# Channel sums of bonus and variance in the recurrent groups: two products with rounded parts in place of one full 32-bit product

## The chip, the cores and the metric

The kernel runs on one core of a Trainium2 chip. The metric is the device time of one execution in microseconds (us). Five engines work side by side, each through a queue of its own in a fixed order: TensorE (PE, matrix products; its weight loads are listed as PEld), VectorE (DVE), ScalarE (ACT), GpSimd (POOL), and SyncE (SP), which here only issues DMAs. Semaphores tie them together.

## The reference, cut to what matters

One decoder layer over 1024 tokens of 1024 channels, all in 32-bit floats: three token mixers on one projection, gates, and a gated feed-forward part with a convolution. The change lies in the recurrent mixer, with 16 heads of 64 channels:

```python
y = rwkv7_scan(rh, wh, kh, vh, -kk, kk * ah)
mu = jnp.mean(y, axis=-1, keepdims=True)
var = jnp.mean(jnp.square(y - mu), axis=-1, keepdims=True)
y = ((y - mu) * lax.rsqrt(var + LNX_EPS)).reshape(B, S, RWKV_WIDTH)
y = y * ln_x_w.astype(f32) + ln_x_b.astype(f32)
bonus = jnp.sum(rh * kh * r_k.astype(f32), axis=-1, keepdims=True) * vh
y = y + bonus.reshape(B, S, RWKV_WIDTH)
return y.astype(dt) * g
```

Two sums over the 64 channels of a head occur for every token: that of `rh * kh * r_k` (the bonus) and that of the squares of the centred `y` (the variance).

## The kernel before, in words

Channels lie on the 128 partitions, tokens along the free axis, so a tile holds two heads, and a sum over a head's channels that is spread back to all of them is a matrix product with `bonesr`, a 128x128 matrix of ones in two 64x64 blocks. It is written once as rounded floats (type fp32r, `FR`). `bones` is the same memory read as full 32-bit floats.

Projections use a split. A 32-bit operand is written as a rounded high part (a copy into an fp32r tile) and a low part (the operand less the high part, again fp32r), and `mm3` (L167 to L169) makes three rounded products of the four parts. Weights are split as they arrive: `whi` on ACT (L128), `wlo` on POOL (L131). A projection block is 2 halves of 512 tokens times 8 channel chunks times 3, that is 48 products of 128x512.

The recurrent mixer runs as four groups (0 to 3) of two tiles `i`, four heads, each. In a group `rwkv_group` does the following. (a) It computes gates (`psu`), sums of the squared keys (`square_sums`, tile `sp` in the buffer with tag `NT`, product `phd` with `bonesr`, already in high and low parts), decays, and the scaled keys and queries. (b) Products `ps` between them for all 16 chunks of 64 tokens, copied and masked out of PSUM by ACT and DVE. Between the two tiles' products the function `bonus` is called for both tiles: product `pbo` of `t0_` (the first half of the tile `kv`, in which the products r, k and r_k stand) with the ones, multiplied with the values on DVE (L514), shifted on ACT (L515), written to memory as `d_bv`. Then the scaled keys are transposed (`pt`, L572) into the tile `BKN`, which takes the buffer of `kv` and so must wait until `d_bv` is written. (c) A triangular solve on DVE (L586 to L600), finished on PE (`pz`, `pw`). (d) The scan over 16 chunks, short products (L639) in a chain through DVE and ACT. (e) The next group's keys and values are projected (`group_kv`), and then for each tile the variance: squares on ACT (L706), product `pvar` with the ones (L708), logarithm and exponential on ACT (`rstd`), three DVE operations (L710 to L713), and the result goes to memory as `d_y`.

32 further projection blocks (`fill`) have nothing to do with the groups: their results are spilled, through a staging tile `st` out of a ring of three buffers with tag `st`, to memory, for the stages after the groups. `fill_to` calls them in while a group is being written. Three quarters belong to the groups, eight blocks to the attention stage.

The order in which each engine runs its instructions is set by the scheduler of the Tile framework when the program is built: it takes the instructions as the kernel writes them, the pools' buffers, and waits, and it moves ready projection products in between the others. It is fixed from then on; at run time no engine looks ahead of its queue.

Of the kernel before, what the change touches and what calls it, by code (L numbers as in the profile page):

```python
# [9 lines left out]
F32 = mybir.dt.float32  # L10
FR = mybir.dt.float32r
AF = mybir.ActivationFunctionType
ALU = mybir.AluOpType
# [4 lines left out]
P = 128  # L18
# [5 lines left out]
HALVES = ((0, 512), (512, 512))  # L24
# [20 lines left out]
def trunk_kernel(ctx: ExitStack, tc: tile.TileContext, xT, memT, pvec, w_in, w_kv, w_upd, w_upg,  # L45
                 w_pool, w_ppool, w_pmem, w_prwkv, w_o, w_fup, w_fdn, out):
    nc = tc.nc
    V, A, G, PE, SP = nc.vector, nc.scalar, nc.gpsimd, nc.tensor, nc.sync

    const = ctx.enter_context(tc.tile_pool(name="const", bufs=1))  # L50
    wp = ctx.enter_context(tc.tile_pool(name="wp", bufs=1))
# [22 lines left out]
    def col(name, i):  # L74
        o, w = PV[name]
        return pv[:, o + i:o + i + 1]
# [7 lines left out]
    bonesr = const.tile([P, P], FR, name="bonesr")  # L84
# [2 lines left out]
    G.memset(braw[0:64, 0:64], 1.0)  # L87
    G.memset(braw[64:128, 64:128], 1.0)
    G.tensor_copy(bonesr, braw)
    bones = bonesr.bitcast(F32)  # L90
    cent = const.tile([P, 64], F32, name="cent")
    mstrict = const.tile([P, 64], F32, name="mstrict")
    mincl = const.tile([P, 64], F32, name="mincl")
# [1 line left out]
    for lo in (0, 64):  # L95
        s = slice(lo, lo + 64)
# [3 lines left out]
    for lo in (0, 64):  # L100
        s = slice(lo, lo + 64)
# [18 lines left out]
    def split(src, hi, lo, lo_eng=None):  # L120
        A.copy(hi, src)
        return (lo_eng or V).tensor_tensor(lo, src, hi.bitcast(F32), op=ALU.subtract)
# [80 lines left out]
    def rstd(dst, ps, eps_col, scale=1.0):  # L203
        act(dst, ps, AF.Ln, bias=eps[:, eps_col:eps_col + 1], scale=scale)
        act(dst, dst, AF.Exp, scale=-0.5)
# [9 lines left out]
    rw = rw_ctx.enter_context(tc.tile_pool(name="rw", bufs=1))  # L215
# [7 lines left out]
    for k in range(KC):  # L223
        tag = ("X01", "X11", "HV", "HV")[k // 2]
# [207 lines left out]
    def rwkv_group(g, kv):  # L432
# [13 lines left out]
        for i in range(2):  # L446
            p = 2 * g + i
            uh, ul = load_up2(w_upd[p])
            for t0, _ in HALVES:
                s = slice(t0, t0 + 512)  # L450
                for e, l, dst, b in ((0, ld, tBN[i][:, 0, s], "w0"), (1, la, tHV[:, i, 0, s], "a0")):
                    ps = psg.tile([P, 512], F32, name="psu", tag="g0")
# [7 lines left out]
        def product_bank(name):  # L460

            turn[0] = (turn[0] + 1) % 3
            shape = [P, 4, 2, C]
            return pss.tile(shape, F32, name=name, tag="s") if turn[0] else \
                psk.tile(shape, F32, name=name, tag="k")

        for i in range(2):
            p = 2 * g + i
            t0_, t1_ = kv[i][:, 0], kv[i][:, 1]
# [9 lines left out]
            for t0, _ in HALVES:  # L479
                s = slice(t0, t0 + 512)  # L480
# [26 lines left out]
        def bonus(i):  # L507

            t0_ = kv[i][:, 0]
            for t0, _ in HALVES:  # L510
                s = slice(t0, t0 + 512)
                ps = pss.tile([P, 512], F32, name="pbo", tag="s")
                PE.matmul(ps, bones, t0_[:, s], start=True, stop=True)
                V.tensor_tensor(t0_[:, s], vs[i][:, s], ps, op=ALU.mult)  # L514
            A.activation(t0_, t0_, AF.Identity, bias=col("ln_b", 2 * g + i))  # L515
            SP.dma_start(d_bv[2 * g + i], t0_)
# [4 lines left out]
        NT = rw.tile([P, 2, NCH, C], F32, name="NT", tag="NT")  # L521
        HV = rw.tile([P, 2, NCH, 2, C], F32, name="HV", tag="HV")
        for i in range(2):
            for c0 in (0, 8):
                ps = pss.tile([P, 8, C], F32, name="pv", tag="s")
# [13 lines left out]
        for i in range(2):  # L539
            us = slice(NCH * i, NCH * i + NCH)  # L540
            for c0 in range(0, NCH, 4):
# [4 lines left out]
                ps = product_bank("ps1")  # L546
# [6 lines left out]
                ps = product_bank("ps2")  # L553
# [6 lines left out]
            for b in range(2 if i == 0 else 0):  # L560
                bonus(b)

            n = NCH if i == 0 else 8
# [5 lines left out]
            for c0 in range(0, NCH, 4):  # L569
                ps = pss.tile([P, 4, P], F32, name="pt", tag="s")  # L570
# [18 lines left out]
        for s in range(31):  # L589
            n, m = 31 - s, s + 1  # L590
# [12 lines left out]
        for u0 in (0, 16):  # L603
            us = slice(u0, u0 + 16)
            ps = pss.tile([P, 16, 32], F32, name="pz", tag="s")
# [7 lines left out]
            ps = pss.tile([P, 16, 32], F32, name="pw", tag="s")  # L613
# [7 lines left out]
        for i in range(2):  # L621
            for e in range(2):
                V.tensor_tensor(RB[i][:, e], RB[i][:, e], mincl.unsqueeze(1).broadcast_to([P, NCH, C]),
                                op=ALU.mult)
# [71 lines left out]
        for i in range(2):  # L696
            p = 2 * g + i
            y = AR[:, i, 1]
            gt = rw.tile([P, 2, T], F32, name="gt", tag=tagA[i])
            SP.dma_start(gt[:, 0], d_bv[p])  # L700
            SP.dma_start(gt[:, 1], d_g[p])
            yq = rw.tile([P, T], F32, name="yq", tag=tagC[i])
            for t0, _ in HALVES:
                s = slice(t0, t0 + 512)
                sq = yq[:, s]
                A.activation(sq, y[:, s], AF.Square)  # L706
                ps = pss.tile([P, 512], F32, name="pvar", tag="s")
                PE.matmul(ps, bones, sq, start=True, stop=True)  # L708
                rstd(sq, ps, 2, 1.0 / 64)
                V.tensor_tensor(y[:, s], y[:, s], sq, op=ALU.mult)  # L710
                V.scalar_tensor_tensor(y[:, s], y[:, s], col("ln_w", p), gt[:, 0, s], op0=ALU.mult,
                                       op1=ALU.add)
                V.tensor_tensor(y[:, s], y[:, s], gt[:, 1, s], op=ALU.mult)  # L713
            SP.dma_start(d_y[p], y)
# [17 lines left out]
    for g in range(4):  # L732
        kv = rwkv_group(g, kv)
# [17 lines left out]
    with tc.tile_pool(name="km", bufs=1) as km:  # L751
# [5 lines left out]
        for k in range(KC):  # L757
            sq = km.tile([P, 256], F32, name="msq", tag="msq", bufs=2)
# [24 lines left out]
        for j in range(8):  # L783
            ws = kv_weights(j) if j > 1 else load_w(w_kv[j], KC, c=0)
            ps = gemm(ws, lambda k: (mh[:, k], ml[:, k]), 256)
# [61 lines left out]
    for hd in range(4):  # L847
        for t0, _ in HALVES:
            s = slice(t0, t0 + 512)
# [6 lines left out]
            for u in range(2):  # L856
                ps = psg.tile([P, 2, 256], F32, name="psco", tag="g0")
# [41 lines left out]
    for j in range(8):  # L899
        ws = load_w(w_pmem[j], 4)  # L900
        for n, (t0, _) in enumerate(HALVES):
            s = slice(t0, t0 + 512)
            SP.dma_start(pm[j][n], d_zg[16 + j][:, s])
            act(pm[j][n], pm[j][n], AF.Sigmoid)
            ps = gemm(ws, lambda k: (oh[k][:, s], ol[k][:, s]))
            V.tensor_tensor(pm[j][n], pm[j][n], ps, op=ALU.mult)
    for j in range(8):
# [4 lines left out]
        for n, (t0, _) in enumerate(HALVES):  # L912
            s = slice(t0, t0 + 512)
            ps = gemm(ws, lambda k: (ph_[k][:, s], pl_[k][:, s]))
# [672 lines left out]
```

## Time and profile before

| what | us |
|---|---|
| median of 3 runs (lowest to highest) | 2102.87 (2102.04 to 2109.29) |
| profiled execution, its own time | 2099.71 |
| span of the profiled execution | 2097.7 |
| granted clock of TensorE, mean | 0.992 |
| end of group 3's scan, in the span | 984 |

How to read the rows. A group row is: line, engine, operation, out<-in by the names in the program, shapes, count, then duration in ns as least/median/most, and first and last start in us. A timeline row is: start in us, duration in us, engine, line, operation, tiles, count; in brackets the idle time of the engine before it and what ended that. A row of waits is: who, for whom, us in total, times, longest. PE's products overlap each other in a pipeline: a product's duration is longer than the distance at which the next may start.

### The profile page before, as it was taken

The page shows a single profiled execution, that of the slowest core. Times are in us where ns is not written, and L with a number is a line of the kernel's source. Part 1 is how long each engine was busy: PE and PEld are TensorE (multiplying, and loading weights), DVE is VectorE, ACT ScalarE, POOL GpSimd, SP SyncE. Part 2 cuts the span into 40 slices and gives each one's busy share as a digit, 9 for nine tenths or more (in the row PEclk, how much of TensorE's full clock was granted, in tenths as well). Part 3 has the DMA queues.
Part 4 walks back from the last instruction along what each step waited for, and adds up shares of the span by engine and source line. Part 5 has one row for each costly group of instructions (what it writes and reads, how often), then busy time and mean ns, then how long its engine had stood idle before and what let it go on. Part 6 is the DMA issues. An engine that isn't in the chain of part 4 may idle for free.

```text
span 2097.7 us, 34129 instructions
## 1 busy us (share of the span) xinstructions
PE 2038.1 (97%) x12246; PEld 1564.7 (75%) x12246; DVE 1347.6 (64%) x2159; ACT 1071.2 (51%) x2252; POOL 818.0 (39%) x925
## 2 busy tenths in 40 slices
PE   8999999999999999999999999999999999999997
PEld 5777766776767667776878887777788777777886
DVE  6567437664558346734695542668777777777798
ACT  7585347623763358434566344545444444444644
POOL 5521212121122121111122355555778888842341
PEclk9999999999999999999999999999999999999999
DMA  4312212120212021212526443634322222159776
GB/s 154 128 41 74 66 58 65 61 82 21 86 61 85 30 83 51 80 62 80 199 88 198 143 146 104 217 108 144 97 87 80 75 85 79 61 171 277 167 181 153
DMA packets 176713, 221.83 MB, mean 106 GB/s; under 512 B 16544, under 2 KB 128288, under 8 KB 176544
## 3 DMA queue, kind: packets, MB, share of 16 engines
q1 hardware_dynamic: 163616, 204.44, 30.1%
q0 software_dynamic: 11856, 14.16, 4.2%
q8 instruction: 97, 1.59, 0.3%
q10 hardware_dynamic: 1072, 1.05, 0.1%
q14 instruction: 72, 0.59, 0.1%
HBM read 170.30 MB, written 49.28 MB: 105 GB/s over the span
## 4 chain that ended last, share of the span: by engine, by line
PE 26%; DVE 7%; POOL 6%; DMA 6%; issue 4%; ACT 3%; SPq 1%; POOLq 0%; ACTq 0%; DVEq 0%
PE psg L169 5%; PE psg L167 5%; PE psg L168 5%; POOL wt L1025 3%; PE psd L168 2%; PE psd L169 2%; PE psd L167 2%; POOL wlo L131 2%; PE psf L169 1%; POOL sm L1010 1%; PE psf L168 1%; PE psf L167 1%; DMA a<-in_w_fup 1%; ACT d L1041 1%; DMA R<-d_f 1%
## 5 line engine op out<-in xcount | busy, mean ns | idle before, releaser
L131 POOL TENSOR_TENSOR wlo<-wraw,whi 128x256 fp32r<-128x256 f32 x480 | 420.1, 885 | 953.0 <-ACT whi L128 822.0
L169 PE MATMUL psg<-hh,wlo 128*128 128x512 f32 x928 | 380.7, 410 | 7.4 <-POOL wlo L131 7.1
L167 PE MATMUL psg<-hh,whi 128*128 128x512 f32 x928 | 383.1, 413 | 0.0
L168 PE MATMUL psg<-hl,whi 128*128 128x512 f32 x928 | 377.8, 407 | 0.0
L128 ACT CAST whi<-wraw 128x256 fp32r<-128x256 f32 x472 | 182.7, 403 | 237.1 <-PE psg L168 114.2
L169 PEld LDWEIGHTS psg<-hh,wlo 128*128 128x128 f32 x928 | 174.9, 188 | 55.2 <-POOL wlo L131 14.2
L167 PEld LDWEIGHTS psg<-hh,whi 128*128 128x128 f32 x928 | 175.3, 189 | 41.8 <-issue 1.7
L168 PEld LDWEIGHTS psg<-hl,whi 128*128 128x128 f32 x928 | 175.4, 189 | 41.1 <-issue 2.2
L1025 POOL TENSOR_TENSOR wt<-a,wt 128x256 fp32r<-128x256 f32 x136 | 134.5, 1017 | 27.8 <-ACT wt L1024 27.8
L167 PE MATMUL psd<-f,u 128*128 128x512 f32 x292 | 115.7, 397 | 5.5 <-ACT f L1325 3.7
L168 PE MATMUL psd<-f,u 128*128 128x512 f32 x292 | 115.2, 395 | 0.7 <-DVE f L1329 0.7
L169 PE MATMUL psd<-f,u 128*128 128x512 f32 x292 | 114.5, 393 | 0.0
L1025 POOL TENSOR_TENSOR wt<-sm,wt 128x256 fp32r<-128x256 f32 x102 | 106.9, 1068 | 15.7 <-ACT wt L1024 15.7
L169 PE MATMUL psf<-h2h,wt 128*128 128x512 f32 x272 | 107.9, 397 | 0.1
L168 PE MATMUL psf<-h2l,wt 128*128 128x512 f32 x272 | 106.9, 393 | 0.0
L167 PE MATMUL psf<-h2h,wt 128*128 128x512 f32 x272 | 106.7, 392 | 0.0
L1024 ACT CAST wt<-sm 128x256 fp32r<-128x256 f32 x102 | 38.0, 404 | 130.5 <-POOL sm L1010 125.8
L1043 DVE SCALAR_TENSOR_TENSOR d<-z,pv,d 128x1023 f32<-128x1023 f32 x68 | 91.6, 1347 | 12.0 <-ACT d L1041 9.5
L169 PE MATMUL psf<-t,wt 128*128 128x512 f32 x204 | 81.3, 399 | 2.2 <-POOL wt L1025 2.1
L168 PE MATMUL psf<-t,wt 128*128 128x512 f32 x204 | 80.3, 394 | 0.0
L167 PE MATMUL psf<-t,wt 128*128 128x512 f32 x204 | 80.2, 393 | 0.0
L683 DVE TENSOR_TENSOR HV<-ph,Hd 64x128 f32<-64x128 f32 x112 | 32.3, 288 | 71.5 <-PE ph L639 47.6
(422 smaller groups left out, 4739.5 us busy)
## 6 DMA issues: line engine op xcount, KB each, us to landing
wraw<-in_w_in SPq DMA_DIRECT2D x240, 128.0 KB, 2.4
a<-in_w_fup SPq DMA_DIRECT2D x128, 128.0 KB, 2.4
d_zg<-st SPq DMA_DIRECT2D x48, 256.0 KB, 2.7
wraw<-in_w_fup SPq DMA_DIRECT2D x80, 128.0 KB, 2.4
fw<-in_w_fdn SPq DMA_DIRECT2D x33, 256.0 KB, 4.4
fraw<-d_f SPq DMA_DIRECT2D x33, 256.0 KB, 5.3
wraw<-in_w_prwkv SPq DMA_DIRECT2D x64, 128.0 KB, 2.4
wraw<-in_w_o SPq DMA_DIRECT2D x64, 128.0 KB, 2.6
```

The costliest lines, as they stand in the source:

```text
L128: A.copy(hi, src)
L131: (V if lo_on_dve[0] else G).tensor_tensor(lo, src, hi.bitcast(F32), op=ALU.subtract)
L167: first = PE.matmul(ps, wh, xh, start=start, stop=False)
L168: PE.matmul(ps, wh, xl, start=False, stop=False)
L169: last_mm[0] = PE.matmul(ps, wl, xh, start=False, stop=stop).ins
L683: ready = V.tensor_tensor(HV[q, :, c + 1, e], ph[q], Hd[q], op=ALU.add).ins
L1010: eng.tensor_tensor(out_[u], a[u], b[u], op=op)
L1024: A.copy(w[0][:, us], src[u])
L1025: last_low[0] = G.tensor_tensor(w[1][:, us], src[u], w[0][:, us].bitcast(F32), op=ALU.subtract).ins
L1041: A.activation(d, z, AF.Identity, scale=col("cw2", j), bias=col("cb", j))
L1043: V.scalar_tensor_tensor(d[:, n:], z[:, :T - n], col(cw, j), d[:, n:], op0=ALU.mult, op1=ALU.add)
```

## The change

Both sums are written as two products with `bonesr`, one of a rounded high part and one of the rounded remainder, added in PSUM. For the bonus a cast on ACT makes the high part and a subtraction on POOL the low one (tiles both named `bh`, from the ring of buffers `st`); for the variance ACT squares twice, once into the rounded tile and once into the 32-bit one, and DVE subtracts. The rounded squares `sv` lie in the one buffer with tag `NT`, which a group's scan uses before and the next group's `sp` after them.

```diff
-    bones = bonesr.bitcast(F32)
...
             for t0, _ in HALVES:
                 s = slice(t0, t0 + 512)
                 ps = pss.tile([P, 512], F32, name="pbo", tag="s")
-                PE.matmul(ps, bones, t0_[:, s], start=True, stop=True)
+                bh, bl = (wp.tile([P, 512], FR, name="bh", tag="st", bufs=3) for _ in range(2))
+                split(t0_[:, s], bh, bl, G)
+                PE.matmul(ps, bonesr, bh, start=True, stop=False)
+                PE.matmul(ps, bonesr, bl, start=False, stop=True)
                 V.tensor_tensor(t0_[:, s], vs[i][:, s], ps, op=ALU.mult)
...
-            for t0, _ in HALVES:
+            sv = rw.tile([P, 2, 2, 512], FR, name="sv", tag="NT")
+            for n, (t0, _) in enumerate(HALVES):
                 s = slice(t0, t0 + 512)
                 sq = yq[:, s]
+                A.activation(sv[:, n, 0], y[:, s], AF.Square)
                 A.activation(sq, y[:, s], AF.Square)
+                V.tensor_tensor(sv[:, n, 1], sq, sv[:, n, 0].bitcast(F32), op=ALU.subtract)
                 ps = pss.tile([P, 512], F32, name="pvar", tag="s")
-                PE.matmul(ps, bones, sq, start=True, stop=True)
+                PE.matmul(ps, bonesr, sv[:, n, 0], start=True, stop=False)
+                PE.matmul(ps, bonesr, sv[:, n, 1], start=False, stop=True)
                 rstd(sq, ps, 2, 1.0 / 64)
```

The scheduler lays a different order for it from the first bonus on. Lines move by a few numbers in the changed kernel: L166 to L168 are now the three products of `mm3`, L130 the weight's low part, L120 and L121 the cast and the subtraction of `split`, L551 and L558 the products `ps`, L574 the transposes.

On PE, around the bonus of group 1. Before, each product is one row (two in the trace), and the operand `kv` has lain ready since the keys were scaled; the fourth follows one row later:

```order
L556 MATMUL ps_3596<-AR,BK_3174 128x128 x4
L513 MATMUL pbo<-kv_2801,bonesr 128x512
L549 MATMUL ps_3665<-AR,BK_3175 128x128
L169 MATMUL psg<-hh,wlo 128x512
L167 MATMUL psg<-hh,whi 128x512
L168 MATMUL psg<-hl,whi 128x512
L169 MATMUL psg<-hh,wlo 128x512
L513 MATMUL pbo<-kv_2801,bonesr 128x512
L513 MATMUL pbo<-kv_2964,bonesr 128x512
L556 MATMUL ps_3689<-AR,BK_3175 128x128
```

Now, with the engine whose semaphore a row waits for in brackets:

```order
L514 MATMUL pbo<-bh,bonesr 128x512 [waits DVE_49,Activation_49]
L515 MATMUL pbo<-bh,bonesr 128x512
L558 MATMUL ps_3743<-AR,BK_3209 128x128 [waits DVE_49]
L558 MATMUL ps_3743<-AR,BK_3209 128x128 x2
L514 MATMUL pbo<-bh,bonesr 128x512 [waits DVE_49,Activation_49]
L515 MATMUL pbo<-bh,bonesr 128x512 [waits Pool_49]
L558 MATMUL ps_3743<-AR,BK_3209 128x128
L514 MATMUL pbo<-bh,bonesr 128x512 [waits DVE_49,Activation_49]
L515 MATMUL pbo<-bh,bonesr 128x512 [waits Pool_49]
```

After these stand six projection products, then the fourth pair, which waits for POOL as well. In group 0 nine projection products stand between the pairs, in group 3 none: there the four pairs follow one another directly.

On POOL at the same place, where before only weight parts stood:

```order
L130 TENSOR_TENSOR wlo<-wraw,whi 128x256 [waits DMAHW5_49,PE_49,Activation_49]
L130 TENSOR_TENSOR wlo<-wraw,whi 128x256 [waits DMAHW0_49,PE_49,Activation_49]
L121 TENSOR_TENSOR bh<-kv_2821,bh 128x512 [waits PE_49]
L121 TENSOR_TENSOR bh<-kv_2984,bh 128x512 [waits PE_49,Activation_49,Pool_49] x2
L130 TENSOR_TENSOR wlo<-wraw,whi 128x256 [waits DMAHW4_49,PE_49,Activation_49]
```

The first subtraction of the group (not shown) stands eight weight parts earlier; the other three wait for PE to have read a buffer of the ring. In group 0 one weight part stands between the last two.

On DVE, between group 1 and group 2, before: the two halves of the next group's key squares (`sp`, L425) partly ahead of the variance operations, the two tiles' operations mixed:

```order
L425 TENSOR_TENSOR sp<-tHV,sp 128x512 x2
...
L710 TENSOR_TENSOR AR<-AR,yq 128x512
L711 SCALAR_TENSOR_TENSOR AR<-AR,pv,gt 128x512
L713 TENSOR_TENSOR AR<-AR,gt 128x512
L710 TENSOR_TENSOR AR<-AR,yq 128x512 x2
L711 SCALAR_TENSOR_TENSOR AR<-AR,pv,gt 128x512 x2
L713 TENSOR_TENSOR AR<-AR,gt 128x512 x2
L710 TENSOR_TENSOR AR<-AR,yq 128x512
L425 TENSOR_TENSOR sp<-tHV,sp 128x512
```

Now, where L711 is the new subtraction and L716 to L719 the former L710 to L713:

```order
L711 TENSOR_TENSOR sv<-yq,sv 128x512 x2
...
L716 TENSOR_TENSOR AR<-AR,yq 128x512 x2
L717 SCALAR_TENSOR_TENSOR AR<-AR,pv,gt 128x512 x2
L719 TENSOR_TENSOR AR<-AR,gt 128x512 x2
L711 TENSOR_TENSOR sv<-yq,sv 128x512 x2
L716 TENSOR_TENSOR AR<-AR,yq 128x512 x2
L717 SCALAR_TENSOR_TENSOR AR<-AR,pv,gt 128x512 x2
L719 TENSOR_TENSOR AR<-AR,gt 128x512 x2
L424 TENSOR_TENSOR sp<-tHV,sp 128x512
```

The tiles now come one after the other, and the key squares after both. On PE, 24 projection products now stand between the end of the scan and the first variance product (54 before; the others moved ahead, 26 of them to before the solve's products `pz`), 22 projection products, four `psu` and the second tile's two high products between the first tile's variance products and the second tile's first low one, and the first key-square product `phd` follows 19 projection products and four `psu` later. After group 3 the variance products stand among projection products.

## The prediction

> **What bounds the kernel now.** I read the page first (busy time by engine, then the chain that ended last), then busy time by stretch over one recurrent group, then the rows of the tiles the change touches, and last the timeline around them.
>
> ```profile
> PE 2038.1 (97%) x12246; PEld 1564.7 (75%) x12246; DVE 1347.6 (64%) x2159; ACT 1071.2 (51%) x2252; POOL 818.0 (39%) x925
> PE 26%; DVE 7%; POOL 6%; DMA 6%; issue 4%; ACT 3%; SPq 1%; POOLq 0%; ACTq 0%; DVEq 0%
> ```
>
> TensorE (PE) has work for 97% of the span; the longest other one, VectorE (DVE), for 64%. A stretch of the recurrent part shows what that means there. Columns: stretch, length, busy us of PE, PE's weight loads, DVE, ScalarE (ACT) and GpSimd (POOL), then granted clock, DMA share and GB/s. The rows run from the end of one group's scan to the end of the next one's.
>
> ```profile
> 320.00:330.00 10.00, 9.89 (x36) 6.43 (x35) 4.16 (x8) 6.22 (x13) 2.94 (x4) 1.00 0.20 59
> 330.00:340.00 10.00, 9.61 (x40) 6.78 (x40) 10.00 (x14) 8.06 (x13) 1.58 (x2) 1.00 0.30 118
> 360.00:370.00 10.00, 7.64 (x32) 5.57 (x31) 7.74 (x8) 6.92 (x9) 5.52 (x5) 1.00 0.36 99
> 380.00:390.00 10.00, 9.43 (x66) 7.38 (x66) 6.98 (x16) 8.25 (x26) 0.55 (x1) 1.00 0.05 15
> 390.00:400.00 10.00, 10.00 (x51) 6.63 (x49) 6.12 (x12) 4.48 (x9) 0.00 (x0) 1.00 0.26 106
> 413.00:453.00 40.00, 40.00 (x173) 32.15 (x172) 36.81 (x76) 10.14 (x22) 11.12 (x14) 1.00 0.29 96
> ```
>
> PE hardly rests: the prepared projection products fill every hole. Even the triangular solve, which looks like DVE's stage, waits for PE:
>
> ```profile
> 451.71 0.86 DVE L600 COPY NT<-tb 32x512 f32<-32x512 f32 x2
> 459.96 1.20 PE L608 MATMUL pz<-tb,NT 32*32 32x32 f32 x64
> ```
>
> DVE puts its result down at 452.57, and the product that reads it starts at 459.96, because projections stand ahead of it in PE's queue. So outside the scan a group lasts as long as PE's own work plus PE's stops. A microsecond less of PE work is a microsecond gained; a stop of PE is one lost, since PE executes in order and nothing later makes it good.
>
> **The product terms: gained.** Old and new form:
>
> ```profile
> L513 PE MATMUL pbo<-kv,bonesr x32: 590/592/697, 160.9 to 844.3; 128*128 128x512 f32 x32
> L708 PE MATMUL pvar<-yq,bonesr x32: 590/592/697, 324.8 to 988.2; 128*128 128x512 f32 x32
> 984.90 1.88 PE L708 MATMUL pvar<-yq,bonesr 128*128 128x512 f32 x4
> 989.08 0.39 PE L168 MATMUL psg<-hl,whi 128*128 128x512 f32 x1
> 989.31 0.40 PE L169 MATMUL psg<-hh,wlo 128*128 128x512 f32 x1
> L428 PE MATMUL phd<-sp,bonesr x16: 392/392/503, 107.7 to 800.7; 128*128 128x512 f32 x16
> ```
>
> Each 32-bit product of 512 columns shows as two rows: 32 rows are 16 products for the bonus and 16 for the variance. A duration includes the pipeline, so I price by distance between starts: four rows in 1.88 us, the last lasting 0.59, are (1.88-0.59)/3 = 0.43 apiece, 0.86 a product. A rounded product (L428 is one with this same matrix) takes a place every 0.23 (989.08 to 989.31), 0.466 for two. Gain: 32 x (0.86-0.466) = 12.6 us, 0.6% of the span, if PE never stops for it.
>
> [...]
>
> **The bonus: what PE now waits for.** The new form needs a cast on ACT and a subtraction on POOL per product. Rows nearest to them:
>
> ```profile
> L121 ACT CAST qh<-q x8: 619/622/632, 1044.6 to 1109.8; 128x512 fp32r<-128x512 f32 x8
> L1329 POOL TENSOR_TENSOR u<-Q,u x12: 1285/1296/3245, 1954.4 to 2043.5; 128x512 fp32r<-128x512 f32 x12
> L1329 POOL TENSOR_TENSOR u<-Q,u 128x512 fp32r<-128x512 f32 x12 | 19.4, 1613 | 46.5 <-ACT u L1325 46.5
> 356.67 8.11 POOL L131 TENSOR_TENSOR wlo<-wraw,whi 128x256 fp32r<-128x256 f32 x6 [20.87 <-ACT whi L128]
> 367.77 0.74 POOL L131 TENSOR_TENSOR wlo<-wraw,whi 128x256 fp32r<-128x256 f32 x1 [2.99 <-ACT whi L128]
> 364.12 1.74 DVE L498 TENSOR_TENSOR tHV<-tHV,kv 128x1024 f32<-128x1024 f32 x1
> 367.11 0.74 DVE L314 SCALAR_TENSOR_TENSOR AR<-psg,pv,AR 128x511 f32<-128x511 f32 x1
> 385.80 1.17 PE L549 MATMUL ps<-AR,BK 64*128 64x128 f32 x9
> ```
>
> Casts: 16 x 0.62 on ACT, which rests more than half of 390 to 400; taken as hidden. Subtractions: 1.30 median, 1.61 mean; beside DVE work on two SBUF tensors POOL needs 8.11/6 = 1.35 for half the width, against 0.74 alone, so 2.6 is the upper end.
>
> High and low parts come from a ring of three buffers. The first product's pair and the second's high part fill it, so the second subtraction can only begin when PE has read the first high part; the third and fourth follow on POOL one behind the other. From the first high product (0.39 to its end) to the last low one lie three subtractions: 0.39 + 3 x 1.30 + 0.2 for handovers = 4.5 us. PE's own work between is, by the order, seven short products (1.63) plus in group 0 nine projections (2.1) and a product with 0.11, while POOL also does a weight part (0.74); in groups 1 and 2 six projections and four products of (1.17-0.27)/8 = 0.11 (1.85); in group 3 nothing. The stops are 4.5+0.74-3.84 = 1.4, twice 4.5-3.48 = 1.0, and 4.5-1.63 = 2.9: together 6.3. At the mean of 1.61 they grow by 0.9 each to 10.0, at 2.6 by 3.9 each to 21.9. I take 1.5 a subtraction, between median and mean, since here DVE mostly reads PSUM: 8.7. So the bonus alone loses: 6.3 gained, 8.7 paid.
>
> Behind the fourth product the bonus is written to memory, and only then may the transposed keys overwrite its tile. A late bonus holds up those copies (L573), and the three buffers, held from the first cast on, also keep spills of projections waiting. Between nothing and 2 us a group; 0.5 taken, 2 in all.
>
> **The variance: two more links.** ACT squares twice instead of once, DVE subtracts:
>
> ```profile
> L706 ACT ACTIVATE yq<-AR x16: 615/632/641, 312.1 to 985.6; 128x512 f32<-128x512 f32 x16
> L425 DVE TENSOR_TENSOR sp<-tHV,sp x16: 656/693/1234, 93.7 to 787.6; 128x512 fp32r<-128x512 f32 x16
> L199 ACT ACTIVATE yq<-pvar,eps x8: 671/680/688, 326.1 to 553.4; 128x512 f32<-128x512 f32 x8
> L199 ACT ACTIVATE yq<-yq x8: 619/624/632, 326.8 to 554.1; 128x512 f32<-128x512 f32 x8
> L710 DVE TENSOR_TENSOR AR<-AR,yq x16: 679/685/693, 327.5 to 992.4; 128x512 f32<-128x512 f32 x16
> PE psu L453 <- ACT tBN L199: 0.4, 1, 0.4
> ```
>
> That is 16 x 0.63 on ACT and 16 x 0.69 on DVE. Ahead of the first tile's products PE has 24 projections (5.6 us) behind the scan, enough. But the rounded squares share one buffer: the second tile's wait until the first tile's are read, and the next group's key squares wait for the second tile's. By the order DVE makes the second tile's low parts behind six operations of the first tile. From the first tile's products that is two logs and two exponentials (2 x 0.68 + 2 x 0.62 = 2.6), six DVE operations and two subtractions of about 0.69 (5.5): 8.1 us, against 28 products x 0.233 = 6.5 that PE has meanwhile. Short by 1.6. The same step comes again at the key squares; there only the present wait of 0.4 is added, since the table load and the sigmoids lie in that place already. 2.0 a boundary at three boundaries: 6.0, between 0 (enough work, as the order was laid) and 12 (the shortfall in full twice). After group 3 projections stand between all products; nothing counted.
>
> **Sum.** -12.6 + 8.7 + 2 + 6.0 = +4.1 us. The profiled execution took 2099.71 (span 2097.7); with that it would take 2103.8. The median shown is 2102.87, 3.2 above; on it the forecast is 2107.
>
> One stop could move either way and is put at zero:
>
> ```profile
> PE psg L169 <- POOL wlo L131: 2.4, 1, 2.4
> 364.83 0.50 PE L169 MATMUL psg<-hh,wlo 128*128 128x512 f32 x1 [2.35 <-POOL wlo L131]
> ```
>
> Once in groups 1 to 3 PE waits for a weight's low part while DVE slows POOL. The first bonus subtraction now stands in POOL's queue near there: up to 2.6 more three times (+8), or less if the new order spreads these parts (-7).
>
> **Rivals.** First, *the gain shows in full*: the order laid enough projections around each new wait, so only the 12.6 is seen: 2090. For it: PE already covers waits of this kind at the key squares, whose products hardly wait (the L428 rows are 392 at the median). Against: three subtractions in series do not fit into 1.6 to 3.8 us of work. If only the bonus stops stay, it is 2099. From a stop term under 2 in all, it is faster by over 0.5%.
>
> Second, *POOL runs at its slowed price*: at 2.6 a subtraction the sum is -12.6 + 21.9 + 2 + 6 = +17: 2120. For it: DVE does some two-tensor work near the bonus (L623, masking the scores). Against: the slow six lie beside L498 and its like, the quick one of 0.74 beside L314, which reads PSUM, and most of what DVE does around the bonus reads PSUM too. It decides from about 2.0 us a subtraction, where the sum passes +10.5. [...]
>
> Third, *the buffers stall the projections*: PE has two PSUM banks for spilled projections, and a spill waiting for a buffer stops the next one. This wait exists once:
>
> ```profile
> PE psg L167 <- ACT st L324: 2.4, 1, 2.4
> ```
>
> Once a group more would add 10: 2117.
>
> **Chances.** About 0.5% (10.5 us) is what a measurement tells from no change. The forecast, +-7 us around 2107, has 0.55; the full gain 0.12; POOL slowed 0.20; buffers 0.13. The full gain is half faster by 0.5% and half not: 0.07, with 0.05 for a shift of the order that gains elsewhere, as the -7 above: faster 0.12. The last two are mostly slower, and a fifth of the forecast's spread: slower 0.34. Same 0.54. The range leaves out a tenth at either side: from 2094, three quarters of the gain, to 2122, just beyond rival two.
>
> **What would show.** Product gain: 64 rows of 0.39 in place of 64 of 0.59, nothing else changed in PE's matmul count but the order. Bonus stops: waits of pbo's second product for POOL, 1 to 3 us a group, largest in group 3. Boundary: waits of pvar's second product for DVE, and of psu for ACT. POOL's subtraction at 1.3 to 1.6. If those waits are absent, the first rival holds; if the subtraction shows over 2, the second; if PE waits for st, the third. The forecast fails also if the shifted order changes the attention stage after 1000 us, which I put at nothing.

## The result, and the profile after

| | before | after |
|---|---|---|
| median, us | 2102.45 (2099.72 to 2109.29, 4 runs) | 2128.91 (2127.97 to 2129.98, 4 runs) |
| span of the profiled execution, us | 2097.7 | 2126.5 |
| mean granted clock of TensorE | 0.992 | 0.985 |

The ratio is 1.012, 95% interval 1.010 to 1.014: slower by 1.2%, where +0.2% had been forecast. The span grew by 28.8 us, the forecast sum was +4.1.

The page of the changed kernel, busy time and the chain that ended last, then its clock:

```profile
PE 2040.2 (96%) x12246; PEld 1575.9 (74%) x12246; DVE 1362.1 (64%) x2175; ACT 1083.3 (51%) x2284; POOL 838.3 (39%) x941
PE 26%; DVE 7%; DMA 6%; POOL 6%; issue 4%; ACT 3%; SPq 0%; POOLq 0%; ACTq 0%; DVEq 0%
core 0: 2126.5 us, clock 0.985
```

On the whole page hardly anything moved: PE still has work for 96% of the span. The loss lies in a few places, so the next views are of single tiles. The new products and the bonus's subtraction (ns least/median/most):

```profile
L121 POOL TENSOR_TENSOR bh<-kv,bh x16: 1270/1292/2282, 134.6 to 864.4; 128x512 fp32r<-128x512 f32 x16
L514 PE MATMUL pbo<-bh,bonesr x16: 388/482/772, 160.1 to 864.9; 128*128 128x512 f32 x16
L515 PE MATMUL pbo<-bh,bonesr x16: 388/498/796, 160.4 to 865.7; 128*128 128x512 f32 x16
```

```profile
L713 PE MATMUL pvar<-sv,bonesr x16: 390/393/496, 325.1 to 1019.7; 128*128 128x512 f32 x16
L714 PE MATMUL pvar<-sv,bonesr x16: 393/452/500, 325.3 to 1020.6; 128*128 128x512 f32 x16
```

64 rows that can be as short as 0.39, as forecast, and a subtraction at 1.29. The bonus's median of 0.48 to 0.50 is not the clock's doing: in group 1 four of its eight rows last 0.49 to 0.50 at a clock of 1.00. But some rows, all in group 3, last almost 0.8: these ran at a lower clock (0.50 from 860 us on, below). Now PE's waits in the changed kernel (us in total, times, longest; `psg` is a projection product, `pv` the product that centres the values, which ACT copies into `HV`), and behind them the row of the first of these waits before:

```profile
PE psg L166 <- ACT whi L127: 18.7, 10, 4.9
PE pv L530 <- ACT HV L533: 4.0, 1, 4.0
PE pbo L515 <- POOL bh L121: 3.5, 6, 0.9
PE ps L551 <- DVE AR L503: 3.1, 3, 1.1
PE phd L428 <- DVE sp L424: 2.7, 3, 0.9
PE psg L166 <- ACT st L323: 2.3, 1, 2.3
PE pvar L714 <- DVE sv L711: 1.1, 2, 0.5
```

```profile
PE psg L167 <- ACT whi L128: 3.1, 3, 2.7
```

The waits that the forecast was about (pbo, phd, pvar) are there, and small. The large one is for the cast of a weight's high part, which the change does not touch: 18.7 us where 3.1 were. Its two worst cases, 4.9 each, are alike, in groups 1 and 2. The timeline around the first, ACT, then DVE, then PE (start, duration; in brackets the idle time before and what ended it):

```profile
445.75 0.68 ACT L325 ACTIVATE st<-psg,pv 128x512 f32<-128x512 f32 x1
460.09 0.69 ACT L307 ACTIVATE kv<-psg,omu 128x512 f32<-128x512 f32 x1 [13.66 <-DVE NT L602]
461.25 1.01 ACT L127 CAST whi<-wraw 128x256 fp32r<-128x256 f32 x3
...
458.77 1.28 DVE L602 COPY NT<-tb 32x512 f32<-32x512 f32 x3
...
456.40 0.39 PE L168 MATMUL psg<-hh,wlo 128*128 128x512 f32 x1
461.70 0.79 PE L166 MATMUL psg<-hh,whi 128*128 128x512 f32 x1 [4.92 <-ACT whi L127]
```

At the head of ACT's queue stands the copy-out of the next group's key projection (L307). It writes into the buffer in which the triangular solve works, so it waits for the solve's last copies on DVE, for 13.66 us. The weight casts queue behind it, and PE, out of weights, starts nothing between 456.40 and 461.70. In the kernel before, no such copy stands ahead of the solve's end. And the stop costs more than its length. Stretches of 3 us (busy us of PE, weight loads, DVE, ACT, POOL; granted clock; DMA share, GB/s), around this stop and around group 3's bonus:

```profile
455.00:458.00 3.00, 1.78 (x8) 1.12 (x6) 2.91 (x5) 0.00 (x0) 0.00 (x0) 1.00 0.00 0
458.00:461.00 3.00, 0.00 (x0) 0.00 (x0) 2.16 (x6) 0.91 (x2) 0.00 (x0) 0.93 0.00 0
461.00:464.00 3.00, 2.30 (x5) 1.70 (x6) 0.75 (x1) 1.26 (x4) 2.10 (x3) 0.50 0.33 115
464.00:467.00 3.00, 3.00 (x9) 2.32 (x8) 0.00 (x0) 0.99 (x2) 0.73 (x1) 0.50 0.32 103
467.00:470.00 3.00, 3.00 (x14) 2.42 (x13) 0.00 (x0) 0.00 (x0) 0.00 (x0) 0.94 0.40 137
```

```profile
857.00:860.00 3.00, 2.90 (x26) 2.55 (x25) 1.97 (x6) 2.80 (x11) 0.00 (x0) 0.99 0.00 0
860.00:863.00 3.00, 2.70 (x7) 1.29 (x7) 2.25 (x5) 1.96 (x6) 1.30 (x2) 0.50 0.00 0
863.00:866.00 3.00, 2.54 (x5) 1.09 (x6) 1.52 (x3) 1.48 (x3) 2.52 (x2) 0.50 0.00 0
866.00:869.00 3.00, 3.00 (x11) 2.14 (x11) 2.76 (x4) 2.47 (x3) 0.00 (x0) 0.50 0.66 262
869.00:872.00 3.00, 3.00 (x10) 2.31 (x11) 0.92 (x3) 0.85 (x3) 0.00 (x0) 0.50 0.68 262
```

Behind the stop the clock is 0.50: the twelve products from 461.70 on take 5.29 us instead of 12 x 0.233 = 2.80. So this stop costs 5.1 + 2.5 = 7.6 us, and there are two. At group 3's bonus the clock is 0.50 for at least 12 us, though PE is busy for 85 to 100% of them.

How much of PE's time this takes together shows in one long stretch, 300 to 985 us, before, in the full change, and in experiment 5 below:

```profile
300.00:985.00 685.00, 672.41 (x5481) 490.94 (x5480) 389.95 (x789) 362.95 (x776) 131.28 (x159) 1.00 0.20 66
300.00:985.00 685.00, 650.34 (x5174) 485.42 (x5173) 392.98 (x770) 362.71 (x768) 144.67 (x167) 0.97 0.19 63
300.00:985.00 685.00, 669.22 (x5487) 497.39 (x5483) 402.96 (x801) 377.63 (x805) 148.66 (x171) 0.99 0.20 67
```

PE rests for 12.6, 34.7 and 15.8 us of it, and the mean clock is 1.00, 0.97 and 0.99: the full change loses by stops and by the clock, in parts of like size (22 us of rest; 0.03 of 685 is some 20 us, an estimate).

The first variance product of groups 1, 2 and 3 starts at 558.7, 791.1 and 1011.5, and before at 548.7, 773.9 and 984.9: the groups lost 9.8, 7.2 and 9.4 us, and the stages behind them only 2.2.

### The profile page after: what moved, and what is told of

It reads as the page before. It is cut to its first block, busy times and chain, and to the rows that moved or that the text cites. A ratio compares the mean times of both kernels' runs of the same rounds, so it can differ in the third digit from the quotient of the medians.

```text
span 2126.5 us, 34222 instructions
## 1 busy us (share of the span) xinstructions
PE 2040.2 (96%) x12246; PEld 1575.9 (74%) x12246; DVE 1362.1 (64%) x2175; ACT 1083.3 (51%) x2284; POOL 838.3 (39%) x941
## 4 chain that ended last, share of the span: by engine, by line
PE 26%; DVE 7%; DMA 6%; POOL 6%; issue 4%; ACT 3%; SPq 0%; POOLq 0%; ACTq 0%; DVEq 0%
PE psg L168 4%; PE psg L167 4%; PE psg L166 4%; POOL wt L1031 3%; PE psd L168 2%; PE psd L167 2%; PE psd L166 2%; PE psf L168 2%; PE psf L167 2%; PE psf L166 2%; POOL wlo L130 1%; DMA wraw<-in_w_fup 1%; POOL sm L1016 1%; DMA a<-in_w_fup 1%; ACT d L1047 1%
## 5 line engine op out<-in xcount | busy, mean ns | idle before, releaser
L130 POOL TENSOR_TENSOR wlo<-wraw,whi 128x256 fp32r<-128x256 f32 x480 | 418.6, 882 | 931.5 <-ACT whi L127 809.8
L166 PE MATMUL psg<-hh,whi 128*128 128x512 f32 x928 | 386.3, 417 | 12.4 <-ACT whi L127 12.4
L168 PE MATMUL psg<-hh,wlo 128*128 128x512 f32 x928 | 382.8, 413 | 7.9 <-POOL wlo L130 7.6
L166 PEld LDWEIGHTS psg<-hh,whi 128*128 128x128 f32 x928 | 177.7, 192 | 55.5 <-ACT whi L127 14.4
L168 PEld LDWEIGHTS psg<-hh,wlo 128*128 128x128 f32 x928 | 176.8, 190 | 54.2 <-POOL wlo L130 13.7
L166 PE MATMUL psd<-f,u 128*128 128x512 f32 x292 | 115.3, 396 | 6.4 <-ACT u L1331 3.5
L168 PE MATMUL psd<-f,u 128*128 128x512 f32 x292 | 114.8, 394 | 1.0 <-DVE u L1335 1.0
L168 PE MATMUL psf<-h2h,wt 128*128 128x512 f32 x272 | 108.1, 397 | 0.1
L166 PE MATMUL psf<-h2h,wt 128*128 128x512 f32 x272 | 106.7, 392 | 0.0
L168 PE MATMUL psf<-t,wt 128*128 128x512 f32 x204 | 81.2, 398 | 2.0 <-POOL wt L1031 2.0
L166 PE MATMUL psf<-t,wt 128*128 128x512 f32 x204 | 80.2, 393 | 0.0
```

The costliest lines, as they stand in the source:

```text
L130: (V if lo_on_dve[0] else G).tensor_tensor(lo, src, hi.bitcast(F32), op=ALU.subtract)
L166: first = PE.matmul(ps, wh, xh, start=start, stop=False)
L168: last_mm[0] = PE.matmul(ps, wl, xh, start=False, stop=stop).ins
```

## The experiments

Two theories stood at the start: the new fixed order is what costs, or the two parts cost by themselves what their waits and queues take.

**1 and 2: each half alone.** In the first the variance is as before, in the second the bonus.

```diff
 # 1: bonus alone, the variance again (its second square and DVE's subtraction go too)
-                PE.matmul(ps, bonesr, sv[:, n, 0], start=True, stop=False)
-                PE.matmul(ps, bonesr, sv[:, n, 1], start=False, stop=True)
+                PE.matmul(ps, bones, sq, start=True, stop=True)
 # 2: variance alone, the bonus again (its cast and subtraction go too)
-                PE.matmul(ps, bonesr, bh, start=True, stop=False)
-                PE.matmul(ps, bonesr, bl, start=False, stop=True)
+                PE.matmul(ps, bones, t0_[:, s], start=True, stop=True)
```

> Only the bonus in rounded parts; the variance stays one 32-bit product. Order theory (most of the 28.8 us comes from the new fixed order: the next group's key projection stands ahead of the triangular solve's end, its copy-out holds ScalarE's queue for 13.7 us, PE stops for 5.1 us and then runs at a granted clock of 0.50 for some 5.5 us, in groups 1 and 2): this kernel's order has no such copy ahead of the solve's end, so it pays only its own stops: 6.3 gained, and 1.65 + 1.1 + 1.1 + about 3 of stops with some slow clock in group 3: 2100 to 2110 us, ratio 0.999 to 1.004. Price theory (each part costs what it does by itself, POOL's subtraction and the boundary links, and the two parts add up to +26): one of the two single parts is slower by at least 13 us, and the two differences add up to 26 within 6.

> Only the variance in rounded parts; the bonus stays one 32-bit product. Order theory: the key projection isn't ahead of the solve's end here either, so the 5.1 us stops at groups 1 and 2 are absent; what stays is 6.3 gained against the boundary's stops (waits of about 1 us for the psu, ps and whi rows and 2.1 to 2.6 for wlo, at three boundaries, with a slow clock behind them): 2100 to 2112 us. Its difference and that of the bonus alone add up to no more than 14 us, half of the full change's 26. Price theory: the differences add up to 26 within 6.

Measured: bonus alone 2115.14 (ratio 1.0062, 1.0040 to 1.0083), variance alone 2100.06 (0.9993, 0.9980 to 1.0006), before 2101.43. The differences are +13.7 and -1.4, together 12.3 of the full change's 26: the halves don't add up, as the order theory says, though the bonus alone lost more than the 2100 to 2110 that it allowed. That excess has a place. POOL's queue in the bonus alone, ahead of group 1's bonus:

```profile
356.46 4.09 POOL L131 TENSOR_TENSOR wlo<-wraw,whi 128x256 fp32r<-128x256 f32 x3 [20.87 <-ACT whi L128]
360.51 1.29 POOL L122 TENSOR_TENSOR bh<-kv,bh 128x512 fp32r<-128x512 f32 x1
361.76 5.04 POOL L131 TENSOR_TENSOR wlo<-wraw,whi 128x256 fp32r<-128x256 f32 x3
```

And PE's waits for these weight parts in the whole run:

```profile
PE psg L169 <- POOL wlo L131: 19.9, 10, 4.6
```

The group's first bonus subtraction stands between weight parts that PE is already short of. The stop of 2.4 becomes 4.6, in groups 1 to 3.

**3 and 4: the key projection held back.** The full change with the next group's first key projection ordered behind the first `pz` product; in 4 besides with the low parts on DVE.

```diff
 # in group_kv; the products of this block then wait for `behind`
-            in_block(16 + p, shifted(8 + p, t[:, 0]))
+            in_block(16 + p, shifted(8 + p, t[:, 0]), behind=behind)
...
-        nxt = group_kv(g + 1, []) if g < 3 else None
+        nxt = group_kv(g + 1, [], first_pz) if g < 3 else None
 # 4, besides
-                split(t0_[:, s], bh, bl, G)
+                split(t0_[:, s], bh, bl, V)
```

> The full change, and the next group's first key projection is ordered behind the first product that reads the solve's result; nothing else is altered by hand. Order theory: the stops of 5.07 and 5.05 us at 461.7 and 694.5 go, and the 5.5 us at a clock of 0.50 behind each: 2 x 7.8 = 15.6 us less, 2108 to 2118 us. Price theory: the copy-out ahead of the solve's end is a symptom, PE would wait for the solve there in any case: 2124 to 2132 us.

> As the one before with the pinned projection, and the bonus's low parts are subtracted on VectorE (0.69 us each by the rows of its like) in place of GpSimd (1.3). If the serial subtractions on GpSimd are a main cost, this is 4 to 10 us faster than the pinned one (three subtractions in series shrink by 0.6 each in four groups: 7.3 us at most, more with the clock behind). If the order is the main cost, it lies within 4 us of the pinned one.

Measured: 2132.01 (1.0140, 1.0117 to 1.0164) and 2133.99 (1.0146, 1.0120 to 1.0172). My 2108 to 2118 failed. The two stops are gone, but not the time. A wait of PE in experiment 3:

```profile
PE pv L530 <- ACT HV L533: 11.1, 3, 3.7
```

And stretches of 4 us around its group 1's bonus:

```profile
394.00:398.00 4.00, 3.70 (x12) 2.12 (x10) 2.64 (x6) 2.31 (x7) 1.75 (x2) 0.51 0.00 0
398.00:402.00 4.00, 3.50 (x10) 1.88 (x8) 2.76 (x5) 2.93 (x5) 2.08 (x2) 0.50 0.17 66
402.00:406.00 4.00, 4.00 (x15) 3.01 (x14) 2.00 (x2) 1.25 (x3) 0.00 (x0) 0.50 0.82 328
406.00:410.00 4.00, 4.00 (x10) 2.69 (x9) 0.84 (x2) 1.01 (x3) 0.00 (x0) 0.50 0.00 0
```

What only group 3 had in the full change, a wait of almost 4 us at `pv` and a half clock around the bonus, groups 1 and 2 have now too. The rival that was right on the time wasn't on the reason: PE did not have to wait for the solve. Its last copies on DVE end at 465.9, and `pz` starts 7.6 us later (timeline of experiment 3), about as long after as before (452.57 to 459.96). It is the solve's end itself that comes 13.3 us later than before:

```profile
461.36 4.50 DVE L602 COPY NT<-tb 32x512 f32<-32x512 f32 x8
473.48 1.20 PE L610 MATMUL pz<-tb,NT 32*32 32x32 f32 x64
```

In the full change and here PE runs dry ahead of the solve's end and has work to spare behind it. The early key projection was a symptom. And DVE's faster subtraction (0.69 at the median, against POOL's 1.28 in 3) bought nothing here: POOL's price is not the cause of this loss.

What keeps projections from where PE is dry? A spilled projection is copied out through the ring `st`, from which the bonus now takes its parts. The copies of spilled projections on ACT between 345 and 398 us, before:

```profile
L324 ACT COPY st<-psg x2: 577/581/585, 357.6 to 377.7; 128x512 f32<-128x512 f32 x2
```

In the changed kernel and in 3 there is none in this stretch: the first one comes at 400.2 and at 399.7, when the bonus's products are through.

**5, 6 and 7: buffers of their own.** The parts move out of the ring to the place where the second tile's `RB` (the scores `ps` as copied for the scan) will lie. 5 is the full change otherwise, 6 has the low parts on DVE, 7 is 5 without the variance's half.

```diff
-                bh, bl = (wp.tile([P, 512], FR, name="bh", tag="st", bufs=3) for _ in range(2))
+                bh, bl = bb[:, 2 * (t0 > 0)], bb[:, 2 * (t0 > 0) + 1]
...
-        RB = [rw.tile([P, 2, NCH, C], F32, name=f"RB{i}", tag=tagC[i]) for i in range(2)]
+        RB = [rw.tile([P, 2, NCH, C], F32, name="RB0", tag=tagC[0])]
+        bb = rw.tile([P, 4, 512], FR, name="bb", tag=tagC[1])
...     # behind the two bonus calls
+            if i == 0:
+                RB.append(rw.tile([P, 2, NCH, C], F32, name="RB1", tag=tagC[1]))
```

> The full change, with the bonus's high and low parts in buffers of their own (in the place where the second tile's RB will lie) and no longer in the ring of three that the copies of spilled projections use. Its fixed order has the same projections ahead of the solve as the kernel before (1296 products of 512 columns ahead of the first product behind the solve, no key projection pulled ahead), and 23 more ahead of group 3's bonus than the full change. Ring theory (the shared ring is what shifts the order, and the order is what costs): the variance alone measured 2100; the bonus adds 6.3 of gain, its own stops and a POOL queue in front of weight parts: 2096 to 2112 us. Starvation theory (both chains lengthen the stage ahead of the solve and PE runs dry there whatever buffers are used): 2120 to 2132 us, as the full change.

> As the one before, with the bonus's low parts subtracted on VectorE. It takes four subtractions of 1.3 us a group out of GpSimd's queue, where in the bonus-only run one of them stood ahead of a weight's low part and the stop there grew from 2.5 to 4.7 us, three times. Ring theory: 2092 to 2104 us, at least 2 below the same kernel with GpSimd. Starvation theory: no better than 2120.

> Only the bonus in rounded parts, with buffers of their own; the variance as before. With the shared ring this was 2115 us. If the loss of that run came from the ring (the order), it falls to 2096 to 2106; if it came from GpSimd's queue alone (a stop of 4.7 us in place of 2.5 at three weights, and the slow clock behind each), it stays at 2108 to 2118.

Measured: 2100.89 (0.9996, 0.9982 to 1.0011), 2093.78 (0.9952, 0.9932 to 0.9971) and 2099.78 (0.9984, 0.9971 to 0.9997), before 2101.58. All three as the ring theory said. The full change's +26.5 is gone with nothing altered but the place of the parts, and 6 is the best version found, 0.5% under the kernel before. The new place differs in two ways: spilled projections don't use it, and it holds four parts in place of three. No run tells the two apart, say with a second ring of three. PE's waits for the low parts fall only from 3.5 to 2.4 us (below), so the loss is not paid as parts that wait for each other; what a longer ring would do to the order stays open. Spilled copies between 345 and 398 us in experiment 5:

```profile
L323 ACT COPY st<-psg x2: 564/573/582, 362.0 to 396.1; 128x512 f32<-128x512 f32 x2
```

Its waits of PE for weight parts and for the bonus's low parts:

```profile
PE psg L168 <- POOL wlo L130: 8.3, 10, 1.4
PE psg L166 <- ACT whi L127: 8.0, 8, 3.0
PE pbo L515 <- POOL bb L121: 2.4, 4, 0.7
```

And the two stretches of 4 us in which group 1's bonus begins:

```profile
390.00:394.00 4.00, 4.00 (x26) 3.08 (x26) 2.41 (x6) 2.65 (x9) 0.00 (x0) 1.00 0.00 0
394.00:398.00 4.00, 4.00 (x20) 3.22 (x19) 3.94 (x6) 3.43 (x9) 1.67 (x2) 1.00 0.12 47
```

Two copies go through, PE is busy throughout, no wait in the recurrent groups is over 1.2 (the 3.0 lies at 1443 us), and the clock stays at 1.00 although the same rounded products stand there. That is not so with own buffers in general. Experiment 7 at the same place:

```profile
390.00:394.00 4.00, 4.00 (x24) 3.78 (x24) 1.63 (x4) 2.79 (x10) 0.00 (x0) 0.50 0.00 0
```

There the clock is 0.50 from about 387 to 397 us, behind no stop of over 0.5 us since 367.7, and the kernel is none the slower than before.

With the same 1296 projections ahead of it, group 1's first `pz` starts at 459.9 in 5 and at 460.0 before, in 3 at 473.5: what 3 lost in that group lies ahead of it.

**8: group 3's bonus.** The full change with a 32-bit product for `g == 3` alone.

```diff
+                if g == 3:
+                    PE.matmul(ps, bones, t0_[:, s], start=True, stop=True)
+                else: ...
```

> The full change, but the bonus of group 3 is again one 32-bit product each; groups 0 to 2 keep their order word for word in the counts of projections. In the full change the clock is 0.50 from about 860 to 873 us there, behind a stop of 4.1 us and rounded products with only short products around them. If the stage's length comes from that (stops and slow clock), some 8 to 11 us less than the full change: 2117 to 2121. If it does not matter: 2129 to 2131, the product gain of 1.6 lost.

Measured: 2118.06 (1.0068, 1.0048 to 1.0088), 10.9 below the full change, as expected. Where the clock had been 0.50:

```profile
861.00:864.00 3.00, 3.00 (x13) 1.71 (x12) 2.77 (x6) 1.03 (x4) 0.00 (x0) 1.00 0.00 0
864.00:867.00 3.00, 3.00 (x10) 1.34 (x9) 2.56 (x5) 1.38 (x2) 0.00 (x0) 1.00 0.00 0
```

So group 3 holds 11 of the 26, by its stops, its slow clock and the 21 projections that the order moved behind its bonus, which this run does not tell apart; 2 x 7.6 for the stops of groups 1 and 2 is most of the rest.

**9 and 10: the ring without rounding.** The variance rounded; the bonus one 32-bit product, but of a plain copy of a plain copy, in 9 in the ring, in 10 in buffers of their own.

```diff
 # bh and bl are F32 tiles here
-                split(t0_[:, s], bh, bl, G)
-                PE.matmul(ps, bonesr, bh, start=True, stop=False)
-                PE.matmul(ps, bonesr, bl, start=False, stop=True)
+                A.copy(bh, t0_[:, s])
+                G.tensor_scalar(bl, bh, 1.0, 0.0, op0=ALU.mult, op1=ALU.add)
+                PE.matmul(ps, bones, bl, start=True, stop=True)
```

> The converse of the buffer test, with no rounding in the bonus: the variance in rounded parts as in the change, the bonus one 32-bit product each that reads a copy of a copy (one copy on ScalarE, one on GpSimd, both plain 32-bit), and both copies lie in the ring of three that the spilled projections use. Ring theory: the order shifts as in the full change (a key projection pulled ahead between the two products behind the solve, no projections ahead of group 3's bonus), and the time is 2112 to 2132 us. If the rounded products themselves cost the time (weaker clock by less work on PE), it stays at 2098 to 2108, as the variance alone (2100) and some waits.

> The control of the one before: the same two plain copies and the same 32-bit product, but the copies lie in buffers of their own. Ring theory: the order stays as before's, 2098 to 2108 us, at least 10 below the one in the ring. If the copies' time in the queues of ScalarE and GpSimd is what costs, both runs lie within 4 us of each other.

Measured: 2114.3 (1.0044, 1.0027 to 1.0061) and 2103.21 (1.0002, 0.9990 to 1.0014). The ring costs 11 us with no rounded product in the bonus; the rest of the 28 came only with the rounded parts, by which step was not separated (the key projection stands between the two `pz` products here, not ahead of both). Group 3 shows the same wait as the full change (longest 4.4), and ahead of group 2's bonus, at 627.2, the clock is 0.50 here too, so that is not a matter of rounded products as such:

```profile
PE pv L531 <- ACT HV L534: 5.0, 3, 4.4
620.00:624.00 4.00, 4.00 (x15) 2.78 (x16) 1.71 (x5) 1.89 (x6) 0.00 (x0) 0.50 0.00 0
```

The twelve executions of 9 run from 2102.64 to 2121.21 us, and the time goes with the clock: the three with a mean clock of 0.991 took 2102.64, 2103.49 and 2108.37, the three with 0.982 to 0.985 took 2116.63 to 2121.21. The order is the same in all of them, so it does not fix the loss by itself.

**11: the bonus's half of the best version.** As 6, with the variance as before.

> Only the bonus in rounded parts, in buffers of their own, low parts on VectorE; the variance one 32-bit product. It tells what the variance's half is worth beside the best version (2093.8 with both). If the variance's gain of 6.3 is eaten by its boundary (the variance alone measured 1.4 below before, the forecast said 6.3 gained and 6.0 paid): 2091 to 2098. If the variance carries the gain: 2098 to 2102.

Measured: 2098.52 (0.9975, 0.9958 to 0.9992), 4.7 above 6, and 3.9 by what each gained on the kernel before in its own round. The intervals overlap (0.9958 to 0.9971), so what the variance's half is worth beside it is not settled.

**12: late casts in the ring.** Experiment 5 changed two things: whose the buffers are, and how early they fill.

```diff
-                split(t0_[:, s], bh, bl, G)
 # hv_read[0]: the last copy-out of `pv`
+                later(A.copy(bh, t0_[:, s]), hv_read[0])
+                G.tensor_tensor(bl, t0_[:, s], bh.bitcast(F32), op=ALU.subtract)
```

> The full change with the shared ring, but each bonus cast is ordered behind the last copy-out of the centred values (pv), so that the ring's buffers are filled about as late as the own buffers were in the run that took the parts out of the ring (first cast at 383 us in place of 363). That run changed two things at once, whose buffers they are and how early they fill. Ring theory (buffers are handed out in the order in which the program is written, so the copies of projections written behind the bonus wait for its parts however late these are made): the order is the shifted one (key projection ahead of the solve's end in groups 1 and 2, none of the 23 projections ahead of group 3's bonus), 2116 to 2132 us. Early-cast theory (casts and subtractions standing early in the queues, and buffers held 33 us, are what costs): 2098 to 2108 us.

Measured: 2133.44 (1.0168, 1.0152 to 1.0184), above even the upper end (five executions, 2121.54 to 2139.25). The casts came late, and still no spilled copy went through between 345 and 398 us:

```profile
L513 ACT CAST bh<-kv x4: 617/622/623, 385.9 to 396.4; 128x512 fp32r<-128x512 f32 x4
```

That fits a ring whose buffers are handed out as the program is written: the bonus is written ahead of the group's `fill_to`, so the fill's copies get their buffers behind it, however late the bonus fills its own.

The table sets the fixed orders beside the times: projection products of 512 columns ahead of group 1's first `pz` product and ahead of group 3's first bonus product, and spilled copies between 345 and 398 us.

| kernel | ahead of `pz` 1 | ahead of bonus 3 | copies | us |
|---|---|---|---|---|
| before | 1296 | 2212 | 2 | 2102.5 |
| 2 variance alone | 1296 | 2229 | 1 | 2100.1 |
| 1 bonus alone | 1307 | 2208 | 1 | 2115.1 |
| full change | 1322 | 2208 | 0 | 2128.9 |
| 3 key projection held back | 1296 | 2208 | 0 | 2132.0 |
| 12 late casts | 1329 | 2208 | 0 | 2133.4 |
| 9 plain copies in the ring | 1319 | 2208 | 0 | 2114.3 |
| 10 plain copies, own buffers | 1296 | 2231 | 2 | 2103.2 |
| 5 own buffers | 1296 | 2231 | 2 | 2100.9 |
| 6 own buffers, DVE | 1296 | 2231 | 2 | 2093.8 |
| 4 as 3, DVE | 1296 | 2208 | 0 | 2134.0 |
| 8 group 3 in 32 bits | 1322 | 2229 | 0 | 2118.1 |
| 7 bonus alone, own buffers | 1296 | 2213 | 2 | 2099.8 |
| 11 bonus alone, own buffers, DVE | 1296 | 2213 | 2 | 2098.5 |

Every kernel with group 3's bonus parts in the ring has 2208, and all of them are slower than before. No column gives the time by itself: 3 has the 1296 of before and is among the slowest, the 2212 of before is four off 2208, and 2 has one copy with no part in the ring. What carries the cause is the three pairs that differ in the buffers alone: full change and 5, 1 and 7, 9 and 10. The ring costs 28.0, 15.4 and 11.1 us in them.

## Why the prediction was wrong, point by point

- **The product gain, 12.6: right.** The rows are 0.39 as forecast. With the ring, POOL's queue and most stops out of the way (6) 7.8 of it reach the end.
- **The bonus stops, 8.7: right in size.** From the first to the last bonus product PE took 2.4, 2.1, 2.2 and 3.5 us more than its own work there at full clock, together 10.2. The waits for POOL among them are only 3.5, in six places, 0.5 to 1.3 a group and smallest in group 3, where the forecast had them largest. There the four pairs do follow one another directly, but at a clock of 0.50 (products 0.6 to 0.9 us apart), which the forecast did not have: that its 3.5 for this group came out is luck. The subtraction's 1.29 excludes the second rival, and the ring's holes the first.
- **Buffers, "0.5 taken, 2 in all": the step that failed.** The sentence named the cause (buffers held from the first cast on keep spills waiting), and the third rival priced it at 10, as a PE wait for `st` once more a group. The runs put 28 us there (2128.9 against 2100.9, the parts' buffers the only difference). It could not be found where the forecast said to look, since PE's wait for `st` stayed at one of 2.3. The likely reason, which the counts fit and no run shows directly, is that the scheduler knew of the blocked ring when it laid the order, and placed the projections elsewhere. So the blockage shows not as a wait for the buffer but as a hole ahead of the solve's end, work to spare behind it, and waits of untouched instructions (`whi`, `pv`).
- **The shifted order had no price.** The forecast reported 24 projections behind the scan and saw the order move, and used it only to fill gaps. The copy-out pulled ahead of the solve's end, 13.7 us at the head of ACT's queue, was readable in the order before any run: it writes into a buffer that the solve holds. Experiment 3 shows, though, that mending it alone gains nothing. "Fill every hole" was too strong for the forecast's own rows: PE is busy for 7.64 of the 10 us from 360 to 370, ahead of the solve.
- **The slow clock was left out.** A stop was priced at its length. Behind the 5 us stops another half is lost (2.5 us behind 5.1), and around a bonus without projections 12 to 16 us run at a clock of 0.50. At the 4.9 us stop it was 0.50, by the rows of 3 us, from about 460.6 to 467.4, and PE stood still for the first 1.1 us of it. What sets this length, and why the clock stayed at 0.50 for 12 to 16 us where PE was busy with short products, no run shows.
- **The variance's boundary, 6.0: about right.** Alone it measured -1.4 net, so of 6.3 gained some 4.9 were paid, 2.1 to 7.6 by the interval.
- **The weight's low part, put at zero: right only by chance.** In the bonus alone it grew by 2.2 in three groups, near the "2.6 more three times" of the text. In the full change the order had moved, and the total is 12.1 against 11.1 us.

Without the ring the forecast's other terms, -12.6 + 8.7 + 6.0, make +2.1; own buffers measured -0.7 (interval -3.8 to +2.3).

## What to carry to other kernels

A small temporary taken from a ring that background work also uses is not free because the ring looks idle: ask in which order its buffers are handed out, and what work is then kept from the places where the main engine runs dry. When an order is laid at build time such a conflict can show in counts of moved work and not as a wait for the buffer, so compare those counts first and price each instruction that moved to the head of an in-order queue (13.7 us at the head of ACT's here). And price a stop of TensorE of about 5 us at one and a half times its length, as here (7.6 for 5.1), because of the clock behind it (0.50 here).

## What the runs showed of the hardware that I had not expected

The granted clock of PE can stay at 0.50 for 12 us (860 to 872 in the full change) and 16 us (394 to 410 in experiment 3) while PE is busy for 85 to 100% of the time. Both stretches have short products and the bonus pairs with stops between them. A stop of about 4 us lies some 11 us ahead of each, but the clock was back at 0.99 to 1.00 in between. Around the same pairs it stayed at 1.00 in experiment 5 and was 0.50 for some 10 us in 7, both with own buffers, and in 9 it was 0.50 from 616 to 628 us with 32-bit products. So it needs neither the ring nor the rounded products; what keeps it down was not separated.
